# Weight sums moved from GpSimd to VectorE, and the modulation dots dealt anew, in a two-layer diffusion step

## The chip, the cores and the metric

One core of a Trainium2 chip runs the whole program. The metric is the device time of one execution in microseconds (us). Five engines work beside each other, each through its own queue in program order: TensorE (PE, with its weight loads as PEld), VectorE (DVE), ScalarE (ACT), GpSimd (POOL) and SyncE (SP, which only issues transfers here).

## The reference

Two layers are applied to 640 tokens of width 1024: 128 context tokens and 512 latent tokens, which differ in their conditioning vector. Each layer is a SwiGLU feed-forward network (FFN) with half weight, a token mixer of four branches (pooling, spatial gating, latent attention, short convolution), and a second FFN:

```python
def swiglu(h, w_gu, w_dn):
    g, u = jnp.split(h @ w_gu, 2, axis=-1)
    return (jax.nn.silu(g) * u) @ w_dn

def layer(x, cond, l, P, ctx, rope):
    mods = (jax.nn.silu(cond) @ P['w_mod'][l] + P['b_mod'][l]).reshape(Bc, N_MOD, 1, D_MODEL)
    ...
    f = swiglu(pre(x, 0), P['w_ffn_gu'][l, 0], P['w_ffn_dn'][l, 0])
    x = x + 0.5 * mods[:, 2] * rmsnorm(f, P['g_post'][l, 0])
    ...
```

`mods` are nine vectors of 1024 per layer and kind of token: scales, shifts and gains. Their matrix `w_mod` is 1024 x 9216 per layer. The hidden width of an FFN is 2816, which is 22 chunks of 128. Everything is float32.

## The kernel before

**Number format.** A float32 operand is split into two parts, h and lo (`split`, L240 to L243): ScalarE casts it to h (L242), VectorE subtracts h from it to get lo (L243). A product is then three matmuls: h by h, lo by h, h by lo. Weights are split as they stream in, so each weight tile costs a cast on ScalarE and a subtraction on VectorE. The halves are called wh and wl for weights, and the FFN's hidden values are split in the same way into `act`.

**An FFN.** The 22 chunks are worked in four parts (`PARTS`: 5, 5, 6, 6). The first part computes gate and up for each chunk by plain products (`gate`, `up`). The chunks of the other parts, but for the last two, are `block` tasks (L648): 15 in each of the four FFNs, 60 in all, in runs of 5, 6 and 4. After each of the first three parts come eight `down` tasks (L799 to L809), one for each 128 output columns: the part's hidden values times the down weights, copied out by ScalarE (L804) and added to a buffer in DRAM by a GpSimd transfer (L806, L808). `before` is the place in the list at which the first part's downs end; these eight are called the first downs here, the sixteen others the later downs.

**A block.** Gate and up for both halves of the tokens would be eight half-size products; a block does seven (Strassen's scheme). The operands' sums S1 to S4 are made once per FFN (`sums` at L627, during the end of the first part and the first downs). The weights' sums are made for every block: from the gate weights g and the up weights u, tiles of 128x1024, four adds of 128x512:

```python
add(t[:, one], g[:, one], u[:, one])          # L236
add(t[:, two], t[:, one], u[:, two])          # L237
add(u[:, one], u[:, one], u[:, two])          # L238
add(g[:, two], g[:, two], e["t"][:, two])     # L220
```

They run on GpSimd. A block's weights are four pieces, split in the order b (g as loaded), t (the tile `wt`), u (the tile `ru` after L238) and 4 (the second half of g after L220). L220 is issued behind the split of b, since that split reads g as loaded. The other three (method `sums`, L227) are issued behind the split of u of the block before, if the next g and u have been fetched by then, or else just ahead of the split of b. `make_piece` (L203) issues all of this; `advance` runs it ahead of the use: within block n the pieces of block n+1 are split, and the sums of block n+2 are made.

A block's TensorE order is: X from b; ScalarE copies X into Z (L672); Y from S1 and t; X from S2; Z from b's second half; X from S3 and u; Y from S4; X from the piece 4. Each is twelve matmuls of 320 columns. X, Z and Y are PSUM tiles; there are four such tiles. VectorE's order within the block, beside the splits, is: L682 (gate, first half), L684, the block's dots, L688 and L689 (up, first half, from Y), L693 and L694 (second half). The split of the finished hidden values is put off until after the next block's first product.

**Dots.** `w_mod` is not multiplied on TensorE, but for a few columns at the start: 128 of its columns at a time are loaded as a tile `wm` of 512 KB, and VectorE takes a product-and-sum of it with each of the two conditioning vectors (`dots`, L371, L375). Such a pair of passes is called a dot here. 96 dots are dealt over the tasks of the four FFNs (32, 28, 28 and 8). At L828 each kind of task has a room, L829 scales the first downs' room, and L833 gives each task its share of the FFN's dots by rounding the running sum. A task issues its dots after its own work (`side`); a block issues them between L684 and L688 (`mod_steps(sides[j])`, L686). The loads run two dots ahead in three buffers, issued by SP (L369) in one queue with the weight loads (L194, L195, L199); a load into a buffer waits there for the dot that read it last.

Of the kernel before, what the change touches and what calls it, by code (L numbers as in the profile page):

```python
# [80 lines left out]
class Kernel:  # L81
# [121 lines left out]
    def make_piece(self, p):  # L203

        nc = self.nc
        e = p.env
        g, u = e["g"], e["u"]
        one, two = slice(0, HK), slice(HK, 2 * HK)
        add = nc.gpsimd.tensor_add
        if p.kind == "4":  # L210
            h, lo = (self.fp.tile([P, HK], F32R, tag=t, name=self.nm(t)) for t in ("wh2", "wl2"))
            self.split(h, lo, g[:, two])
            return h, lo
        if p.kind == "b":
            self.sums(p)
        h = self.unit_tile(False, 2 * HK, F32R, "wh")
        lo = self.unit_tile(False, 2 * HK, F32R, "wl")
        self.split(h, lo, {"b": g, "t": e["t"], "u": u}[p.kind])
        if p.kind == "b":
            add(g[:, two], g[:, two], e["t"][:, two])  # L220
        if p.kind == "u":
            for q in self.streams[False]["raw"]:
                if isinstance(q, Piece) and q.kind == "b":
                    self.sums(q)
        return h, lo

    def sums(self, p):  # L227

        e = p.env
        if "t" in e:  # L230
            return
        g, u = e["g"], e["u"]
        one, two = slice(0, HK), slice(HK, 2 * HK)
        add = self.nc.gpsimd.tensor_add
        t = e["t"] = self.fp.tile([P, 2 * HK], F32, tag="wt", name=self.nm("wt"))
        add(t[:, one], g[:, one], u[:, one])  # L236
        add(t[:, two], t[:, one], u[:, two])  # L237
        add(u[:, one], u[:, one], u[:, two])  # L238
# [352 lines left out]
    def ffn(self, l, st, mod_todo, first=False):  # L591

        a, nc = self.a, self.nc
# [13 lines left out]
        def spill():  # L607

            nc.gpsimd.dma_start(self.d_x, self.x)
            self.gens["sums"] = sums()  # L610
# [155 lines left out]
        mid = []  # L766
        if first:
            def first_fn(*ws):
                p = [self.ps() for _ in ws]
                self.projs(list(zip(p, ws)), KC, self.h, (0, 1), hook=self.first_hook)  # L770
                self.advance(False, 5)
                self.st.close()
                begin()
                self.gens["sums"] = sums()
                new_act(0)
                gate_out(0, p[0], (0, 1))
                up_out(0, p[1], (0, 1))
                gate_out(1, p[2], (0, 1))
            mid.append(Task("first", first_fn, (wg[0, 0], wg[0, 1], wg[1, 0]), ahead=0))
            mid.append(up(1, 1, (0, 1)))  # L780
# [3 lines left out]
        for part, nj in enumerate(PARTS):  # L784
# [26 lines left out]
            before = before or len(mid)  # L811
# [13 lines left out]
            return Task("down2", fn, (wd[c][:, j0 * P:NJ * P],))  # L825


        room = {"gate": 1.4, "up": 1.4, "down": 1.0, "block": 1.0}  # L828
        rooms = [room.get(t.name, 0.0) * (0.3 if t.name == "down" and i < before else 1.0) for i, t in enumerate(mid)]  # L829
        done, n = 0.0, 0  # L830
        for t, x in zip(mid, rooms):
            done += x
# [592 lines left out]
    def build(self):  # L1425
# [6 lines left out]
        def start():  # L1432
# [77 lines left out]
            def squares():  # L1510
                sums = (acc, self.s6())
                for c in range(KC):
                    q = sums[c] if c < 2 else self.t6()
                    nc.scalar.activation(q, self.x[:, c, :], AF.Square)
                    if c > 1:
                        nc.vector.tensor_add(sums[c % 2], sums[c % 2], q)
                nc.vector.tensor_add(acc, *sums)
# [199 lines left out]
```

## Time and profile before

| | |
|---|---|
| Three timed runs | 3231.4, 3232.16, 3234.57 us; median 3232.16 |
| The profiled execution | 3228.82 us |
| its span, first to last instruction | 3227.0 us |
| Busy: TensorE | 3042.9 us, 94% |
| Busy: VectorE | 2334.3 us, 72% |
| Busy: ScalarE | 1436.4 us, 45% |
| Busy: GpSimd | 1079.7 us, 33% |
| TensorE's granted clock, mean | 0.981 of full speed |

Durations and waits below are of the profiled execution. A row of a wait names who stood, at which line, for whom, and how long. A matmul's time of 0.31 us includes its way through the array; such matmuls start about 0.147 us apart.

### The profile page before, as it was taken

The page shows a single profiled execution, that of the slowest core. Times are in us where ns is not written, and L with a number is a line of the kernel's source. Part 1 is how long each engine was busy: PE and PEld are TensorE (multiplying, and loading weights), DVE is VectorE, ACT ScalarE, POOL GpSimd, SP SyncE. Part 2 cuts the span into 40 slices and gives each one's busy share as a digit, 9 for nine tenths or more (in the row PEclk, how much of TensorE's full clock was granted, in tenths as well). Part 3 has the DMA queues.
Part 4 walks back from the last instruction along what each step waited for, and adds up shares of the span by engine and source line. Part 5 has one row for each costly group of instructions (what it writes and reads, how often), then busy time and mean ns, then how long its engine had stood idle before and what let it go on. Part 6 is the DMA issues. An engine that isn't in the chain of part 4 may idle for free. (4 is left out here: it accounts for less than half of the span.)

```text
span 3227.0 us, 51500 instructions
## 1 busy us (share of the span) xinstructions
PE 3042.9 (94%) x20278; PEld 2986.2 (93%) x20278; DVE 2334.3 (72%) x3282; ACT 1436.4 (45%) x2535; POOL 1079.7 (33%) x841
## 2 busy tenths in 40 slices
PE   7999998999999989999989999989999999899997
PEld 6999998899999979999979999979999998899997
DVE  7878768876666597787686788678666666866665
ACT  4344356454432354343554343564444324544344
POOL 4245344500011244354444354344000113343344
PEclk9999999999999999999999999999999999999999
DMA  4436653311234444536544436542111444345344
GB/s 178 166 110 186 165 169 119 133 58 60 68 112 148 154 150 158 158 118 175 181 152 157 151 119 179 180 152 93 60 55 61 144 140 163 139 133 140 104 130 153
DMA packets 140213, 433.45 MB, mean 134 GB/s; under 512 B 16834, under 2 KB 34050, under 8 KB 139076
## 3 DMA queue, kind: packets, MB, share of 16 engines
q1 hardware_dynamic: 119380, 351.34, 32.6%
q0 software_dynamic: 20304, 78.66, 9.1%
q8 instruction: 159, 2.61, 0.3%
q14 instruction: 82, 0.67, 0.1%
q10 hardware_dynamic: 288, 0.17, 0.0%
HBM read 377.51 MB, written 52.59 MB: 133 GB/s over the span
## 5 line engine op out<-in xcount | busy, mean ns | idle before, releaser
L243 DVE TENSOR_TENSOR wl<-raw,wh 128x1024 fp32r<-128x1024 f32 (+3 forms) x525 | 645.0, 1231 | 432.5 <-ACT wh L242 425.2
L311 PE MATMUL ps<-act,wh 128*128 128x320 f32 x2816 | 570.1, 313 | 29.5 <-DVE act L243 10.8
L242 ACT CAST wh<-raw 128x1024 fp32r<-128x1024 f32 (+3 forms) x525 | 481.2, 919 | 78.9 <-PE ps L311 39.1
L311 PEld LDWEIGHTS ps<-act,wh 128*128 128x128 f32 x2816 | 457.7, 190 | 38.2 <-DVE act L243 14.1
L665 PE MATMUL ps<-s,wh 128*128 128x320 f32 x1920 | 445.4, 311 | 26.7 <-DVE t L689 26.7
L375 DVE CUSTOM_DVE_ANT_0 t<-wm,sc,par 128x1024 bf16<-128x1024 f32 x256 | 373.2, 1493 | 10.0 <-DMA wm<-in_w_mod 9.9
L311 PE MATMUL ps<-slotA,wh 128*128 128x320 f32 x1312 | 366.4, 317 | 14.3 <-ACT wh L242 11.7
L311 PE MATMUL ps<-slotD,wh 128*128 128x320 f32 x1312 | 352.4, 316 | 20.7 <-DVE slotD L1528 15.0
L311 PE MATMUL ps<-slotA,wl 128*128 128x320 f32 x1312 | 363.5, 315 | 6.3 <-DVE wl L243 6.0
L311 PE MATMUL ps<-slotB,wh 128*128 128x320 f32 x1312 | 362.2, 314 | 3.0 <-DVE slotB L509 1.6
L311 PE MATMUL ps<-slotC,wh 128*128 128x320 f32 x1312 | 352.5, 317 | 7.1 <-ACT wh L242 3.2
L665 PEld LDWEIGHTS ps<-s,wh 128*128 128x128 f32 x1920 | 327.0, 188 | 32.8 <-ACT ps L672 22.2
L311 PE MATMUL ps<-act,wl 128*128 128x320 f32 x1408 | 355.0, 311 | 0.0
L665 PE MATMUL ps<-s,wl 128*128 128x320 f32 x960 | 298.0, 310 | 1.8 <-DVE wl L243 1.4
L311 PEld LDWEIGHTS ps<-slotD,wh 128*128 128x128 f32 x1312 | 236.9, 193 | 23.9 <-DVE slotD L1528 16.3
L311 PEld LDWEIGHTS ps<-slotA,wh 128*128 128x128 f32 x1312 | 239.1, 192 | 17.4 <-ACT wh L242 12.7
L311 PEld LDWEIGHTS ps<-slotA,wl 128*128 128x128 f32 x1312 | 239.1, 192 | 11.2 <-DVE wl L243 10.0
L311 PEld LDWEIGHTS ps<-act,wl 128*128 128x128 f32 x1408 | 246.9, 190 | 0.2
L311 PEld LDWEIGHTS ps<-slotC,wh 128*128 128x128 f32 x1312 | 236.9, 193 | 9.1 <-ACT wh L242 3.5
L311 PEld LDWEIGHTS ps<-slotB,wh 128*128 128x128 f32 x1312 | 239.0, 192 | 4.7 <-DVE slotB L509 2.1
L311 PE MATMUL ps<-slotC,wl 128*128 128x320 f32 x960 | 240.5, 316 | 1.4 <-DVE wl L243 1.0
L804 ACT COPY s<-ps 128x640 f32<-128x640 f32 x96 | 66.6, 694 | 297.0 <-issue 171.9
(341 smaller groups left out, 6461.9 us busy)
## 6 DMA issues: line engine op xcount, KB each, us to landing
raw<-in_w_gu SPq DMA_DIRECT2D x162, 512.0 KB, 3.8
wm<-in_w_mod SPq DMA_DIRECT2D x144, 512.0 KB, 4.7
raw<-in_w_dn SPq DMA_DIRECT2D x96, 384.0 KB, 3.2
raw<-in_w_gate SPq DMA_DIRECT2D x64, 512.0 KB, 3.6
d_f<-s POOLq DMA_DIRECT2D x96, 320.0 KB, 5.0
ru<-in_w_gu SPq DMA_DIRECT2D x60, 512.0 KB, 4.0
raw<-in_w_in SPq DMA_DIRECT2D x44, 512.0 KB, 3.4
raw<-in_w_dn SPq DMA_DIRECT2D x64, 320.0 KB, 2.9
```

The source lines that it names most:

```text
L242: self.nc.scalar.copy(h, src)
L243: self.nc.vector.tensor_sub(lo, src, h.bitcast(F32))
L311: nc.tensor.matmul(ps[:, hf, :HW], st[:, ws], m[:, k0 + k, hf * HW:(hf + 1) * HW], start=(first and k == 0 and i == 0), stop=(last and k = ...
L375: self.nc.vector.tensor_tensor_reduce(junk, wm, self.sc[:, j, :], 0.5, self.par[l][:, C_BMOD + ch:C_BMOD + ch + 1], ALU.mult, ALU.add, sel ...
L665: nc.tensor.matmul(o, w[x][:, ws], a[y][:, k, :], start=(new and k == 0 and i == 0), stop=(k == n - 1 and i == 2), skip_group_check=not new)
L804: nc.scalar.copy(t.rearrange("p (a b) -> p a b", a=2), ps[:, :, :HW])
```

## The change

The four weight sums of a block go from GpSimd to VectorE; where they are issued does not move. The rooms that deal the dots change: a block's room falls from 1.0 to 0.2, and the factor of the first downs rises from 0.3 to 0.6. The number of dots, their order and their loads stay.

```diff
@@ make_piece
-        add = nc.gpsimd.tensor_add
+        add = nc.vector.tensor_add
@@ sums
-        add = self.nc.gpsimd.tensor_add
+        add = self.nc.vector.tensor_add
@@ ffn
-        room = {"gate": 1.4, "up": 1.4, "down": 1.0, "block": 1.0}
-        rooms = [room.get(t.name, 0.0) * (0.3 if t.name == "down" and i < before else 1.0) for i, t in enumerate(mid)]
+        room = {"gate": 1.4, "up": 1.4, "down": 1.0, "block": 0.2}
+        rooms = [room.get(t.name, 0.0) * (0.6 if t.name == "down" and i < before else 1.0) for i, t in enumerate(mid)]
```

## Rows read from the trace of the kernel before

**Rows 1.** The page's first part: busy time, share of the span, instructions.

```profile
PE 3042.9 (94%) x20278; PEld 2986.2 (93%) x20278; DVE 2334.3 (72%) x3282; ACT 1436.4 (45%) x2535; POOL 1079.7 (33%) x841
```

**Rows 2.** Twelve block stages: window, length; busy PE, PEld, DVE, ACT, POOL; PEclk, DMA, GB/s.

```profile
1861.40:1941.80 80.40, 75.46 (x505) 73.85 (x505) 69.74 (x88) 36.39 (x59) 40.56 (x23) 1.00 0.38 120
...
2866.80:2928.90 62.10, 62.02 (x423) 61.64 (x422) 46.45 (x57) 30.16 (x49) 27.26 (x19) 1.00 0.26 83
...
sum 777.90, PE 749.31 PEld 740.65 DVE 639.62 ACT 362.93 POOL 368.64; mean PE 62.44 PEld 61.72 DVE 53.30 ACT 30.24 POOL 30.72
```

**Rows 3.** ScalarE's timeline, last FFN: start, length, what; two copies L672, one block apart.

```profile
2893.74 0.41 ACT L672 COPY ps<-ps 128x320 f32<-128x320 f32 x1 [0.81 <-PE ps L665]
...
2906.06 0.41 ACT L672 COPY ps<-ps 128x320 f32<-128x320 f32 x1 [0.81 <-PE ps L665]
```

**Rows 4.** TensorE's waits: total us, times, longest.

```profile
PE ps L665 <- DVE t L689: 26.7, 23, 2.4
```

**Rows 5.** VectorE's timeline in a block with a dot.

```profile
1389.09 1.27 DVE L375 CUSTOM_DVE_ANT_0 t<-wm,sc,par 128x1024 bf16<-128x1024 f32 x1
...
1390.29 2.30 DVE L375 CUSTOM_DVE_ANT_0 t<-wm,sc,par 128x1024 bf16<-128x1024 f32 x1
...
1393.05 0.49 DVE L689 TENSOR_TENSOR t<-t,ps 128x320 f32<-128x320 f32 x1
...
1395.23 1.07 DVE L694 TENSOR_TENSOR t<-t,t 128x320 f32<-128x320 f32 x1
...
1396.23 0.68 DVE L243 TENSOR_TENSOR wl<-raw,wh 128x512 fp32r<-128x512 f32 x1
...
1397.10 0.82 DVE L243 TENSOR_TENSOR act<-t,act 128x640 fp32r<-128x640 f32 x1 [0.19 <-ACT act L242]
```

**Rows 6.** TensorE's and GpSimd's timeline at the same place.

```profile
1393.68 0.39 PE L665 MATMUL ps<-s,wh 128*128 128x320 f32 x1 [2.39 <-DVE t L689]
...
1391.59 2.13 POOL L237 TENSOR_TENSOR wt<-wt,ru 128x512 f32<-128x512 f32 x1
```

**Rows 7.** Groups by form, GpSimd: busy, mean ns, idle before; two of four sums.

```profile
L237 POOL TENSOR_TENSOR wt<-wt,ru 128x512 f32<-128x512 f32 x60 | 129.0, 2149 | 4.7
...
L220 POOL TENSOR_TENSOR raw<-raw,wt 128x512 f32<-128x512 f32 x60 | 87.5, 1458 | 178.1 <-DVE wl L243 111.8 <-issue 66.4
```

**Rows 8.** VectorE's timeline in a first down, GpSimd idle: two passes of a dot.

```profile
1264.68 1.28 DVE L375 CUSTOM_DVE_ANT_0 t<-wm,sc,par 128x1024 bf16<-128x1024 f32 x1
...
1265.89 1.28 DVE L375 CUSTOM_DVE_ANT_0 t<-wm,sc,par 128x1024 bf16<-128x1024 f32 x1
```

**Rows 9.** Two lines by source: shortest, median, longest ns, then first and last start.

```profile
L694 DVE TENSOR_TENSOR t<-t,t x60: 491/1071/1078, 189.0 to 3135.6; 128x320 f32<-128x320 f32 x60
...
L243 DVE TENSOR_TENSOR wl<-ru,wh x60: 1212/1352/2603, 174.2 to 3121.8; 128x1024 fp32r<-128x1024 f32 x60
```

**Rows 10.** Three down stages by window, columns as in the block stages: first, then later.

```profile
1235.70:1275.50 39.80, 37.10 (x242) 36.58 (x241) 22.75 (x31) 14.62 (x22) 13.81 (x13) 0.96 0.53 184
...
1340.60:1375.80 35.20, 35.20 (x242) 35.20 (x242) 26.87 (x37) 11.79 (x17) 11.83 (x10) 1.00 0.85 243
...
1456.00:1498.20 42.20, 42.20 (x290) 42.20 (x289) 29.31 (x39) 12.32 (x17) 13.53 (x11) 1.00 0.77 213
```

**Rows 11.** First FFN, gates and ups: window; then timelines at its first down.

```profile
88.00:132.00 44.00, 44.00 (x302) 44.00 (x301) 42.81 (x57) 13.94 (x19) 10.61 (x5) 1.00 0.42 135
...
138.03 0.81 DVE L243 TENSOR_TENSOR act<-t,act 128x640 fp32r<-128x640 f32 x1
...
138.90 0.90 PE L311 MATMUL ps<-act,wh 128*128 128x320 f32 x2 [4.39 <-DVE act L243]
```

**Rows 12.** Transfers 1340 to 1376 us: KB, us to landing; then VectorE's idle before L375.

```profile
wm<-in_w_mod SPq DMA_DIRECT2D x7, 512.0 KB, 5.7
...
  DMA wm<-in_w_mod: 9.9, 10
```

## The prediction, made before the changed kernel ran

> **What bounds the kernel now.** I read the page's busy line first: TensorE is busy for 94% of the span, VectorE for 72%, GpSimd for 33% [rows 1]. So time can be won only where TensorE stands, and the next view is the table by stage over the twelve stretches of block products (four FFNs, three parts each, 60 blocks). They last 777.9 us together; the shortest one of five blocks lasts 62.1 us, the longest one of six 80.4 us [rows 2]. What a block costs without a stop is read from ScalarE's timeline: its copy of X into Z (L672) comes once a block, and two such copies lie 2906.06 - 2893.74 = 12.32 us apart where no dot is near [rows 3]. 60 x 12.32 = 739.2 us, so 777.9 - 739.2 = 38.7 us is all that the blocks have to give. Of it, 26.7 us is one wait by name: TensorE on VectorE's L689, 23 times, 1.16 us each [rows 4].
>
> One dotted block shows why. VectorE begins the two passes of a dot at 1389.09; the first takes 1.27 us, the second 2.30 us, and L689 comes only at 1393.05 [rows 5]. TensorE, which had ended the last product of the block and the X product of the next, stands 2.39 us for L689, since the next Y is written into the PSUM tile that L689 reads [rows 6]. The second pass is long because GpSimd is inside a weight sum (L237) during it [rows 6]. The same slowing shows wherever VectorE reads two SBUF operands while GpSimd adds: L694 takes 0.49 us at least and 1.07 us in the median, a split of 1024 columns 1.21 us at least and up to 2.60 us [rows 9]. The four sums of a block take 1.46 to 2.15 us each on GpSimd, some 7 us together (the longest and the shortest of the four in [rows 7]).
>
> **The change part by part.** *Dots.* From the rooms at L828 and L829 and the rounding at L833, the 96 dots of all four FFNs are dealt so (before to after): gates and ups of the first FFN 7 to 9, first downs 7 to 19, blocks 38 to 12, later downs 44 to 56. By FFN the blocks go 11, 12, 12, 3 to 4, 4, 4, 0. No two of the 12 are in neighbouring blocks, and three are in the last block of a part, where no next Y waits: nine are left that can make one wait.
>
> *Sums.* Four adds of 128x512 go from GpSimd to VectorE, 240 in all. The trace has no such add on VectorE; the nearest row is the split of the same 512 columns with two fp32 SBUF inputs, 0.68 us [rows 5]. An instruction holds VectorE some 0.07 us less than it lasts: passes of 1.28 us start 1.21 us apart [rows 8]. So an add costs 0.61 us. The bounds are 0.61 and, if something still slowed it as L694 is slowed, 0.61 x 1.07/0.49 = 1.3 us; I take 0.61, because the thing that slowed L694 is exactly what leaves.
>
> *VectorE's load in a block afterwards,* with undisturbed durations: three splits of 1024 at 1.14 (1.21 less 0.07 [rows 9]), one of 512 at 0.61, the act split of 640 at 0.75, five passes over PSUM at 0.42 (L689's 0.49 less 0.07) and L694 at 0.42 [rows 5, 9]: 7.3 us. Four adds: 2.4 us, and 0.1 us by estimate for the one that reads its forerunner. Sum 9.8 of 12.32 us. A dot is 2 x 1.21 + 0.08 = 2.5 us [rows 8]; a dotted block has 12.3 of 12.32 us, so it just fits, and its neighbours take up what is late.
>
> *What is queued behind the adds.* Three of them (L236 to L238) stand behind the split of u and ahead of L693, L694 and the w4 split; the fourth (L220) between the split of b and L682. What TensorE needs first is L689, and both places have slack before it: a product is 12.32/7 = 1.76 us, S4 ends 1.76 us before the block does and the next Y starts 1.76 us after, so L688 and L689 (1 us together) may lie 2.5 us late. Without a dot they are on time. With one, adding up the queue (wl of b, L220, L682, L684, wl of t, 2.5 us of dot, L688, L689) brings L689 about 0.7 us too late. The bounds are 0 and the 1.16 us that a wait on L689 takes today [rows 4]. 9 x 0.7 = 6.3 us. L694 also comes about 2 us later, and with it the act split; the downs read act a block later, except behind a part's last block, which has no sums behind it. The adds need their raw and ru tiles landed, or VectorE itself would stand; the loads are issued about one block ahead, and nothing in the trace stands on them.
>
> *Starts of the parts.* Of the 38.7 us, 38.7 - 26.7 = 12 us are not waits on L689: shorter stops at the first block of a part, on splits that come after GpSimd's chain of four sums (some 7 us [rows 7]). On VectorE the chain is 2.5 us, so the splits are ready in time. I leave 1.5 us for all twelve parts; the bounds are 0 and 12.
>
> *Blocks, sum:* 739.2 + 6.3 + 1.5 = 747.0, against 777.9: 30.9 us won.
>
> *Downs.* A later down has 4.4 us (5 chunks) or 5.3 us (6 chunks) of TensorE; VectorE needs 0.75 to 0.9 us for the split and 2.5 us for a dot, at most 3.4 us. Today TensorE never stands in the later downs: busy 35.20 of 35.20 us with VectorE at 26.87 [rows 10]. Two more dots make 31.9 of 35.20. Weights are split two downs ahead, so the single down with two dots is covered by 8.8 us of finished weights. I cost it at nothing; without that cover each extra dot costs its 2.5 us. In the first downs VectorE is busy 22.75 of 39.80 us [rows 10]; four more dots make 32.8. The act split and the operand sums stand ahead of these dots in program order. Nothing.
>
> *Gates and ups of the first FFN.* Here there is no cover. From 88 to 132 us VectorE is busy 42.81 of 44.00 us [rows 11]. Two more dots are 5.0 us, 1.2 us of it fits, 3.8 us is carried along. TensorE has four PSUM tiles and weights two units ahead, so it stands only at the end: the first down already waits 4.39 us for the last act split, which ends at 138.84 [rows 11], and will wait 3.8 us more. Bounds 0 and 5.0.
>
> *DMA.* The same loads, more of them inside the downs: seven wm loads in a later part of 35 us today at 85% share and 243 GB/s [rows 10], each landing 5.7 us after issue [rows 12]; nine would add 1.05 MB, 4.3 us at that rate, against 5.3 us free. A load is issued two dots ahead, so 5.7 us is covered by 8.8 us. SP's queue holds the wm load until an earlier dot has ended, with the raw loads behind it; three raw tiles lie ahead. VectorE stood 9.9 us in all for wm [rows 12]. Nothing, bound 4.3 us in each of the four densest stages.
>
> *Sum:* -30.9 + 3.8 = -27.1 us on the profiled execution of 3228.8 us (span 3227.0), to some 3202. The three timed runs have their median 3.3 us above it; the same step from the median gives 3232.2 - 27 = **3205 us**.
>
> **One rule weighed.** VectorE is busy for 69.74 of 80.40 us in the fullest block stage [rows 2]. The Trainium skill, "Perfetto Trace Analysis", section "Optimizing Scalar/DVE Operations", says that work may be offloaded from a saturated VectorE to ScalarE or even GpSimd, and adds that between VectorE and GpSimd it might not help because they share an SBUF port. The first half speaks against this change and is the third rival below; the trace agrees with the second half, in the 2.30 us pass beside L237.
>
> **The rivals.**
> 1. *The denser downs take part of it back.* If transfers do not keep up, each of the four stages with nine dots grows by 4.3 us: 17 us, 3205 + 17 = 3222 us. For: 85% share. Against: 15% free and two dots of lead. It decides once a load takes over about 8.8 us to land. Chance 0.13.
> 2. *No change.* The twelve dots added to the first downs fall in front of the splits and operand sums that the first block of each part needs: 12 x 2.5 = 30 us, 3235 us, against 3232. For: these stages hold the longest waits for act. Against: 17 us of VectorE's time free there [rows 10]. Chance 0.10.
> 3. *Slower: VectorE becomes the bound in the blocks.* If an add costs 1.2 us there, twice its price (as splits beside GpSimd take twice), a block needs 12.1 of 12.32 us, nothing makes up for a dot (12 x 2.5 = 30 us), and in-order waits of some 0.5 us a block (30 us) come on top: +60 + 3.8 - 38.7 = +25, 3257 us. It decides when VectorE has more than 2.5 us of backlog at L688 block after block. For: 9.8 of 12.32 us leaves little. Against: the 0.68 us row. Chance 0.09.
> 4. *All of it is won* and the gates lose nothing: 3232 - 38.7 = 3193.5 us. Chance 0.08.
>
> **How the numbers follow.** Forecast 0.60 at 3205 (own range 3197 to 3217). The range 3194 to 3227 takes in rival 1, the upper end of rival 4 and the bounds of the dotted blocks, the parts' starts, the gates and the transfers. About 0.2% is what a measurement here can tell from no change. Faster by over 0.2%: forecast, rivals 1 and 4, 0.81; within: rival 2, 0.10; slower: 0.09.
>
> **What would show it.** Right: L689 nearly gone from TensorE's waits, block stages near 62 us (five blocks) and 74.5 (six), splits in blocks near 1.23 us, L694 at 0.49 us, later downs still 35.2 and 42.2 us, the wait of the first down up from 4.4 to some 8 us. Wrong: VectorE's adds well over 0.7 us, waits for splits inside the later downs, VectorE standing on wm or ru, or L689 waits that stay in blocks without a dot.

## The result

The changed kernel takes 3197.89 us in the median (3197.05 to 3201.47), the kernel before 3232.14 us beside it: a ratio of 0.9902, 95% interval 0.9890 to 0.9915, or 34 us less. The forecast was 3205 us, 27 us less, in a range from 3194 to 3227. The profiled execution took 3198.12 us, its span is 3196.3 us, 30.7 us shorter than before.

The twelve block stages of the kernel after, by window (length, then busy PE, PEld, DVE, ACT, POOL, clock, DMA share, GB/s); they answer to [rows 2]:

```profile
1840.10:1914.50 74.40, 74.38 (x506) 73.90 (x505) 62.37 (x93) 36.06 (x59) 0.86 (x1) 1.00 0.35 111
...
2841.30:2902.90 61.60, 61.60 (x422) 61.60 (x421) 47.39 (x70) 29.84 (x49) 0.54 (x1) 1.00 0.23 70
...
sum 743.60, PE 743.04 PEld 739.09 DVE 592.61 ACT 360.29 POOL 14.15; mean PE 61.92 PEld 61.59 DVE 49.38 ACT 30.02 POOL 1.18
```

743.6 us now, 777.9 before. The six-block stage fell from 80.4 to 74.4 us, the undisturbed five-block stage from 62.1 to 61.6. By its records TensorE is busy 743.04 of 743.60 us, but a matmul's record reaches past the start of the next, so that short stands do not show there. ScalarE's copy of X into Z, once a block, shows them (the dot runs between the first two of these copies):

```profile
1380.56 0.41 ACT L672 COPY ps<-ps 128x320 f32<-128x320 f32 x1 [0.81 <-PE ps L665]
...
1392.88 0.41 ACT L672 COPY ps<-ps 128x320 f32<-128x320 f32 x1 [0.81 <-PE ps L665]
...
1405.71 0.41 ACT L672 COPY ps<-ps 128x320 f32<-128x320 f32 x1 [0.81 <-PE ps L665]
```

12.32 us from copy to copy without a dot, 12.83 us behind one. The three stages of the last FFN, whose blocks have no dot now, take 61.6 + 73.9 + 49.3 = 184.8 us, exactly 15 times 12.32. So the 743.6 - 739.2 = 4.4 us that are left lie in the nine stages with dots.

GpSimd went from 368.64 to 14.15 us, and VectorE, which took over 240 adds, is less busy in the blocks than before (592.61 against 639.62 us), partly since 26 dots left them and partly since its instructions got shorter.

The wait of [rows 4] and the forms of VectorE's instructions after (shortest, median, longest in ns; then a group by form with its mean):

```profile
PE ps L665 <- DVE t L689: 0.4, 2, 0.2
...
L694 DVE TENSOR_TENSOR t<-t,t x60: 491/492/494, 191.5 to 3104.7; 128x320 f32<-128x320 f32 x60
...
L243 DVE TENSOR_TENSOR wl<-ru,wh x60: 1218/1226/1228, 177.9 to 3090.8; 128x1024 fp32r<-128x1024 f32 x60
...
L237 DVE TENSOR_TENSOR wt<-wt,ru 128x512 f32<-128x512 f32 x60 | 41.5, 692 | 2.1
```

L689 is waited for twice, 0.4 us in all (23 times and 26.7 us before). L694 takes 0.49 us always (median 1.07 in [rows 9]), the split of `ru` at most 1.23 us (up to 2.60), and an add 0.69 us, against 2.15 us on GpSimd in [rows 7].

A block with a dot, VectorE's timeline, in the same stage as [rows 5] but one block later, down to the next block's sums (L236 to L238):

```profile
1388.15 1.22 DVE L243 TENSOR_TENSOR wl<-wt,wh 128x1024 fp32r<-128x1024 f32 x1
...
1389.28 1.28 DVE L375 CUSTOM_DVE_ANT_0 t<-wm,sc,par 128x1024 bf16<-128x1024 f32 x1
...
1390.49 1.28 DVE L375 CUSTOM_DVE_ANT_0 t<-wm,sc,par 128x1024 bf16<-128x1024 f32 x1
...
1392.22 0.49 DVE L689 TENSOR_TENSOR t<-t,ps 128x320 f32<-128x320 f32 x1
...
1393.77 0.68 DVE L236 TENSOR_TENSOR wt<-raw,ru 128x512 f32<-128x512 f32 x1
...
1394.48 0.69 DVE L237 TENSOR_TENSOR wt<-wt,ru 128x512 f32<-128x512 f32 x1
...
1395.09 0.68 DVE L238 TENSOR_TENSOR ru<-ru 128x512 f32<-128x512 f32 x1
```

Both passes take 1.28 us. L689 ends at 1392.71 us, and TensorE's next Y starts at 1392.86 us, only 0.2 us later than it could have by the pace of its matmuls.

Two down stages after, columns as above, and the wm loads in the first of the two (KB, us to landing); they answer to [rows 10] and [rows 12]:

```profile
1330.80:1366.00 35.20, 35.20 (x243) 35.20 (x242) 30.22 (x50) 11.68 (x17) 5.98 (x7) 1.00 0.92 261
...
1440.70:1482.90 42.20, 42.20 (x290) 42.20 (x289) 35.12 (x55) 12.32 (x17) 6.00 (x7) 1.00 0.90 255
...
wm<-in_w_mod SPq DMA_DIRECT2D x9, 512.0 KB, 8.7
```

TensorE still never stands in them. But the share of the transfers rose from 0.85 to 0.92, and a wm load lands after 8.7 us (5.7 before).

The first FFN's first downs: the stage by window, before and after, then of the kernel after VectorE's timeline (a dot's second pass, the last act split) and TensorE's two stands; they answer to [rows 11]:

```profile
129.90:172.20 42.30, 37.89 (x242) 37.36 (x241) 24.75 (x33) 12.69 (x18) 14.34 (x12) 0.92 0.52 177
...
128.00:176.00 48.00, 38.34 (x242) 37.67 (x241) 37.37 (x58) 15.04 (x22) 7.97 (x9) 0.86 0.60 204
...
122.66 2.60 DVE L375 CUSTOM_DVE_ANT_0 t<-wm,sc,par 128x1024 bf16<-128x1024 f32 x1
...
141.90 0.81 DVE L243 TENSOR_TENSOR act<-t,act 128x640 fp32r<-128x640 f32 x1
...
137.47 0.90 PE L311 MATMUL ps<-act,wh 128*128 128x320 f32 x2 [5.80 <-ACT act L242]
...
142.76 1.43 PE L311 MATMUL ps<-act,wh 128*128 128x320 f32 x4 [3.86 <-DVE act L243]
```

TensorE stands 5.80 us and then 3.86 us, where it stood 4.39 us once. The stage takes 48.0 us; the same matmuls took 42.3 us before.

So the span's 30.7 us are -34.2 us in the blocks, +5.7 us in the first FFN's first downs, and -2.2 us in all other stages together. These 2.2 us are not traced to the change: the start of the first downs alone lies between 128.0 and 130.3 us in the profiles of this study, 130.0 us in the kernel before and in the run with lowered gate rooms.

### The profile page after: what moved, and what is told of

Same layout as the page of the kernel before. It is cut to its first block, busy times and chain, and to the rows that moved or that the text cites. A ratio compares the mean times of both kernels' runs of the same rounds, so it can differ in the third digit from the quotient of the medians.

```text
span 3196.3 us, 51354 instructions
## 1 busy us (share of the span) xinstructions
PE 3036.4 (95%) x20278; PEld 2985.0 (93%) x20278; DVE 2353.4 (74%) x3522; ACT 1432.2 (45%) x2535; POOL 653.7 (20%) x601
## 5 line engine op out<-in xcount | busy, mean ns | idle before, releaser
L243 DVE TENSOR_TENSOR wl<-raw,wh 128x1024 fp32r<-128x1024 f32 (+3 forms) x525 | 601.8, 1148 | 380.2 <-ACT wh L242 371.9
L375 DVE CUSTOM_DVE_ANT_0 t<-wm,sc,par 128x1024 bf16<-128x1024 f32 x256 | 330.2, 1327 | 12.9 <-DMA wm<-in_w_mod 12.5
L311 PEld LDWEIGHTS ps<-slotA,wh 128*128 128x128 f32 x1312 | 240.5, 193 | 19.9 <-ACT wh L242 15.1
L808 POOL DMA_DIRECT2D d_f<-s x64 | 55.3, 864 | 800.4 <-ACT s L804 720.7
```

Of the source, the lines that this page charges most:

```text
L243: self.nc.vector.tensor_sub(lo, src, h.bitcast(F32))
L311: nc.tensor.matmul(ps[:, hf, :HW], st[:, ws], m[:, k0 + k, hf * HW:(hf + 1) * HW], start=(first and k == 0 and i == 0), stop=(last and k = ...
L375: self.nc.vector.tensor_tensor_reduce(junk, wm, self.sc[:, j, :], 0.5, self.par[l][:, C_BMOD + ch:C_BMOD + ch + 1], ALU.mult, ALU.add, sel ...
L808: nc.gpsimd.dma_start(self.d_f[c], t, accum_op=ALU.add)
```

## The experiments

Ratios are to the kernel before, run on the same chip. Edits are shown against the changed kernel; "..." marks what is left out of a line. Where a kernel has lines more than the changed one, its line numbers are shifted, and the text says to what.

**The sums alone.** The dots are dealt as before.

```diff
-        room = {"gate": 1.4, "up": 1.4, "down": 1.0, "block": 0.2}
+        room = {"gate": 1.4, "up": 1.4, "down": 1.0, "block": 1.0}
-  ... * (0.6 if t.name == "down" and i < before else 1.0)
+  ... * (0.3 if t.name == "down" and i < before else 1.0)
```

> Sums on VectorE, dots dealt as before (38 of 96 in blocks). Theory A (both parts are needed: a dotted block fills VectorE, 9.8 + 2.5 of 12.32 us, so dotted blocks in a row pile up and L689 comes late): the blocks win well under the 34 us of the changed kernel, some 10 to 20 us, TensorE waits on L689 in most runs of dotted blocks, some 20 us in all; time about 3215 us. Rival B (GpSimd's adds beside the dots were the whole cause, so that moving them is enough): block stages as in the changed kernel, 744 us together, and the first FFN's gates as in the kernel before; time about 3193 us.

Measured: 3213.26 us, ratio 0.9950 (0.9933 to 0.9966). The blocks take 763.8 us, 14.0 us less than before; the first FFN's first downs 42.1 us, as before. The sum over its block stages, and TensorE's waits:

```profile
sum 763.80, PE 752.10 PEld 739.25 DVE 638.13 ACT 357.18 POOL 14.03; mean PE 62.68 PEld 61.60 DVE 53.18 ACT 29.76 POOL 1.17
```

```profile
PE ps L665 <- DVE t L689: 11.5, 15, 1.0
```

15 waits on L689 are left, up to 1.0 us each; 14 of them stand behind a block with a dot that follows another such block. Theory A holds, B falls: taking GpSimd away does not make 38 dotted blocks free, since a dotted block leaves VectorE late and the next dotted one finds it late.

**The dots alone.** The sums stay on GpSimd.

```diff
-        add = nc.vector.tensor_add
+        add = nc.gpsimd.tensor_add
...
-        add = self.nc.vector.tensor_add
+        add = self.nc.gpsimd.tensor_add
```

> Sums stay on GpSimd, dots dealt as in the changed kernel (12 in blocks). Theory A: a block without a dot runs in 12.32 us beside GpSimd, as it does in the last FFN of the kernel before; nine dots still cost 1.2 us each and the parts' first blocks their stops: blocks about 755 us together (777.9 before), first FFN's first downs 5 to 6 us longer as in the changed kernel; time about 3216 us. Rival B: the blocks stay near 778 us, time about 3236 us.

Measured: 3212.28 us, ratio 0.9946 (0.9931 to 0.9960). The blocks take 757.2 us, 20.6 us less than before; the first FFN's first downs 47.9 us. The sum over its block stages, and TensorE's waits:

```profile
sum 757.20, PE 747.44 PEld 742.28 DVE 602.15 ACT 364.38 POOL 345.66; mean PE 62.29 PEld 61.86 DVE 50.18 ACT 30.36 POOL 28.80
```

```profile
PE ps L665 <- DVE t L689: 7.9, 6, 2.1
```

Six long waits, four of 0.9 and two of 2.1 us, are a part of what the few dots left in the blocks still cost beside GpSimd. In the last FFN, where no block has a dot, the stages take the same 184.8 us as in the changed kernel: beside a block without a dot GpSimd's sums cost nothing here. Theory A again. The two halves won 14.0 and 20.6 us in the blocks, 34.6 together; the whole change won 34.2. They add up, although only 12 blocks with a dot are left for the sums to help, where there were 38; why they still win 13.6 us there is not shown. The loss of 5.7 us comes with the dots alone.

**Fewer dots in the first FFN's gates.**

```diff
-        room = {"gate": 1.4, "up": 1.4, "down": 1.0, "block": 0.2}
+        room = {"gate": 0.3, "up": 0.3, "down": 1.0, "block": 0.2}
-  ... * (0.6 if t.name == "down" and i < before else 1.0)
+  ... * (0.8 if t.name == "down" and i < before else 1.0)
```

> The changed kernel with rooms 0.3 (not 1.4) for gates and ups and 0.8 (not 0.6) for the first downs: the first FFN has 2 dots in its gates and ups instead of 9, none in the last two of them. Theory (the 5.7 us that the first FFN's first downs lost are dots queued ahead of the last act split): that stage falls from 48.0 to about 39 us, as long as in the other FFNs, the rest stays; time about 3189 us. Rival (the stage is longer for the dots dealt to its own downs): no gain or a loss, 3198 us or more, since these downs get 8 dots instead of 5.

Measured: 3189.73 us, ratio 0.9871 (0.9856 to 0.9885). The first downs by window, and the gates ahead of them:

```profile
130.20:165.40 35.20, 35.20 (x242) 35.20 (x241) 32.50 (x51) 12.59 (x18) 3.98 (x7) 1.00 0.70 250
...
88.00:128.00 40.00, 40.00 (x275) 40.00 (x274) 31.56 (x41) 13.28 (x18) 11.03 (x6) 1.00 0.27 87
```

The stage takes 35.2 us, less than the 39 us expected: TensorE does not stand in it at all, though these downs hold eight dots instead of five. In the gates VectorE is busy 31.56 of 40.00 us, where it was 42.81 of 44.00 before. So both stands of that stage, the 4.39 us of the kernel before among them, came from dots queued ahead of the last act split; dots in the downs themselves cost nothing here. The granted clock of the stage is 1.00, where it was 0.92 and 0.86 with the stands.

**No dots in the blocks of the last three FFNs, more in their downs.**

```diff
-        room = {"gate": 1.4, "up": 1.4, "down": 1.0, "block": 0.2}
+        room = {"gate": 1.4, "up": 1.4, "down": 1.0, "block": 0.2 if first else 0.0}
```

> The changed kernel with no dots at all in the blocks of the last three FFNs; their 28, 28 and 8 dots all lie in the downs, 11 in each of the later parts of eight downs with 28, three of them in pairs. Theory (the downs have room and the few dots in the blocks cost almost nothing): within 3 us of the changed kernel, 3195 to 3200 us; later downs 35.2 and 42.2 us as before. Rival (denser downs cost, by VectorE or by transfers): each of the four stages with 11 dots grows by several us, 3205 us or more.

Measured: 3202.25 us, ratio 0.9914 (0.9899 to 0.9929). The downs did keep their 35.2 and 42.2 us, but two of the block stages behind them grew, from 74.7 to 77.2 and from 74.4 to 78.2 us. VectorE at the end of the downs, and TensorE at the start of the first of these stages:

```profile
1362.14 1.29 DVE L375 CUSTOM_DVE_ANT_0 t<-wm,sc,par 128x1024 bf16<-128x1024 f32 x1 [3.04 <-DMA wm<-in_w_mod]
...
1371.90 1.28 DVE L375 CUSTOM_DVE_ANT_0 t<-wm,sc,par 128x1024 bf16<-128x1024 f32 x1
...
1372.04 0.41 PE L665 MATMUL ps<-s,wl 128*128 128x320 f32 x1 [2.25 <-DVE wl L243]
```

VectorE stood 3.04 us for a wm load that had not landed, its remaining dots moved on to the block's start, and TensorE stood 2.25 us for a split. The theory missed by where the price falls: not in the dense downs, but in the first block behind them. Eight fewer dots in the blocks win less than this costs. The two stages that grew are the six-block ones behind downs of 35.2 us; behind the downs of 42.2 us, also with 11 dots, nothing was lost. The interval of the ratio overlaps that of the changed kernel, 4 us apart in the medians, so the reading rests on the two block stages of the profile, +2.5 and +3.8 us.

**Two adds more in each block.** L236 and L237 are issued twice.

```diff
         add(t[:, one], g[:, one], u[:, one])
         add(t[:, two], t[:, one], u[:, two])
+        add(t[:, one], g[:, one], u[:, one])
+        add(t[:, two], t[:, one], u[:, two])
```

> The changed kernel with L236 and L237 issued twice: two adds of 128x512 more on VectorE in each block, 0.61 us each, same result. Theory (a block without a dot needs 9.8 of 12.32 us and L689 may lie 2.5 us late, so 1.3 us more is still covered; only dotted blocks fall behind): block stages 744 to 749 us, time within 5 us of the changed kernel, about 3201 us. Rival (VectorE's queue is already what a block waits for, and every add is paid): 60 x 1.25 = 75 us more, about 3273 us.

Measured: 3222.05 us, ratio 0.9977 (0.9968 to 0.9986), some 24 us more than the changed kernel ((0.9977 - 0.9902) x 3230). The blocks take 768.4 us. Both expectations missed. ScalarE's copy of X into Z (L674 here) in two neighbouring blocks without a dot:

```profile
1433.80 0.41 ACT L674 COPY ps<-ps 128x320 f32<-128x320 f32 x1 [0.81 <-PE ps L667]
...
1446.44 0.41 ACT L674 COPY ps<-ps 128x320 f32<-128x320 f32 x1 [0.81 <-PE ps L667]
```

12.64 us a block, not 12.32, once the first two or three blocks of a part have used up what they were ahead; blocks behind a dot take 14.2 to 15.1 us.

**Four adds more in each block.**

```diff
         add(t[:, one], g[:, one], u[:, one])
         add(t[:, two], t[:, one], u[:, two])
+        add(t[:, one], g[:, one], u[:, one])
+        add(t[:, two], t[:, one], u[:, two])
+        add(t[:, one], g[:, one], u[:, one])
+        add(t[:, two], t[:, one], u[:, two])
```

> The changed kernel with L236 and L237 issued three times: four adds more, 2.5 us a block, so that a block without a dot needs 12.3 of 12.32 us of VectorE. Theory: the point from which VectorE is the bound lies here; the short stands for ScalarE in each block no longer fit, and a dot (2.5 us) is paid in full: 9 x 2.4 us and some 0.2 to 0.5 us in each block, 20 to 50 us more, 3220 to 3250 us, with waits on L689 in most blocks. Rival (VectorE still has room): within 10 us of the changed kernel.

Measured: 3295.53 us, ratio 1.0206 (1.0189 to 1.0223), some 98 us more than the changed kernel, again outside both expectations. The blocks take 840.8 us. The same copy (L676 here), ScalarE's cast of the hidden values with what stands behind it, and TensorE's waits (L681 is L677 of the changed kernel, L688 is L684, L693 is L689, L698 is L694):

```profile
1461.02 0.41 ACT L676 COPY ps<-ps 128x320 f32<-128x320 f32 x1 [0.81 <-PE ps L669]
...
1466.15 0.72 ACT L246 CAST act<-t 128x640 fp32r<-128x640 f32 x1 [4.71 <-DVE t L698]
...
1467.09 0.43 ACT L681 COPY t<-ps 128x320 f32<-128x320 f32 x1
...
1475.12 0.41 ACT L676 COPY ps<-ps 128x320 f32<-128x320 f32 x1 [0.81 <-PE ps L669]
...
PE ps L669 <- ACT t L681: 54.4, 36, 2.7
...
PE ps L669 <- DVE t L688: 11.8, 12, 2.7
...
PE ps L669 <- DVE t L693: 7.5, 9, 1.0
```

14.10 us a block: the last two adds cost 14.10 - 12.64 = 1.46 us, all of their 0.72 us each. Taken back from there, four adds more at 0.72 us leave 14.10 - 2.88 = 11.2 us that VectorE's round of the changed kernel takes, stands included, and two adds on top make 12.66 us, against 12.64 measured. So the slack of an undotted block is some 1.1 us by this estimate, not the 2.5 us of the prediction's sum. And the wait is another one than I had looked for: mostly not L689, but ScalarE's copies. The adds stand ahead of L694; ScalarE's cast of the hidden values waits for L694 (4.71 us), and behind that cast, in ScalarE's queue, stand the copies of Y and X that free X for its third product.

**GpSimd's adds beside VectorE's.** VectorE makes the sums as in the changed kernel; GpSimd makes four adds a block of the same size, into a tile that nothing in the block reads.

```diff
             add(g[:, two], g[:, two], e["t"][:, two])
+            nc.gpsimd.tensor_add(self.wm[:, one], e["t"][:, two], self.sc[:, 0, one])
...
         add(u[:, one], u[:, one], u[:, two])
+        for _ in range(3):
+            self.nc.gpsimd.tensor_add(self.wm[:, one], t[:, two], self.sc[:, 0, one])
```

> The changed kernel, and GpSimd beside it does four adds of 128x512 a block into a tile that nobody reads, on operands of the same size (the sums that are used stay on VectorE). Theory (an add on GpSimd slows whatever reads two SBUF operands on VectorE): splits, sums and dots last up to twice as long while GpSimd is in an add, VectorE needs some 14 of 12.32 us a block, and the blocks become VectorE's: 60 x 1.5 to 2 us more, 3280 to 3320 us. Rival (GpSimd's sums mattered only because their results came late): as the changed kernel, 3198 to 3203 us.

Measured: 3311.60 us, ratio 1.0254 (1.0234 to 1.0275). The blocks take 858.6 us. VectorE's forms (the split of 512, the act split, L220, L694 as L697 here, and L239, which is L238) and GpSimd's adds:

```profile
L246 DVE TENSOR_TENSOR wl<-raw,wh 128x512 fp32r<-128x512 f32 x62 | 94.0, 1517 | 16.6 <-ACT wh L245 16.6
...
L246 DVE TENSOR_TENSOR act<-t,act 128x640 fp32r<-128x640 f32 x65 | 92.8, 1428 | 14.3 <-ACT act L245 14.3
...
L220 DVE TENSOR_TENSOR raw<-raw,wt 128x512 f32<-128x512 f32 x60 | 64.7, 1079 | 2.1
...
L697 DVE TENSOR_TENSOR t<-t,t 128x320 f32<-128x320 f32 x60 | 50.4, 840 | 2.1
...
L239 DVE TENSOR_TENSOR ru<-ru 128x512 f32<-128x512 f32 x60 | 41.0, 684 | 0.0
...
L241 POOL TENSOR_TENSOR wm<-wt,sc 128x512 f32<-128x512 f32 x180 | 296.1, 1645 | 306.8 <-DVE wt L238 297.1
```

The split of 512 columns takes 1.52 us in the mean (0.69 in the changed kernel), the act split 1.43 (0.83), L697 0.84 (0.49), L220 1.08 (0.69); L239, inside which GpSimd's first add starts, keeps its 0.68 us. GpSimd's results are used by nobody in the block, so the lateness of its results is out as a cause: it is the adds as such, beside VectorE, that hold VectorE up. (The added adds also read the tile of the sums, which VectorE overwrites a block later; VectorE never stands for that in this trace.)

**The changed kernel once more, and the operand sums on VectorE too.** The second has the lowered gate rooms of the third experiment, and one line more:

```diff
-                    nc.gpsimd.tensor_add(d, f(self.h[0][:, c, :]), f(self.h[1][:, c, :]))
+                    nc.vector.tensor_add(d, f(self.h[0][:, c, :]), f(self.h[1][:, c, :]))
```

> The changed kernel once more, unaltered, beside the next one on the same chip: 0.990 of the kernel before, some 30 us less.

> The kernel with the gates' rooms lowered, and the operand sums' adds too (L637, 32 of 128x640, at the end of the first part) on VectorE. Theory (a GpSimd add beside VectorE costs VectorE more than VectorE's own add): the weight split ahead of the last act split falls from 1.76 to 0.82 us, the first downs of the last three FFNs from 39.8 to about 37 us; 6 to 12 us less than with the lowered rooms alone, ratio to the kernel before about 0.984. Rival (VectorE's queue in front of the act split grows by the adds): no gain or some us more, ratio 0.988 or above.

Measured: 3196.02 us, ratio 0.9891 (0.9875 to 0.9908) for the changed kernel again; 3178.27 us, ratio 0.9837 (0.9822 to 0.9851) with the operand sums on VectorE.

In the second profile of the changed kernel one six-block stage takes 1.4 us more than in the first. Its window, and VectorE near its start:

```profile
1840.64:1916.50 75.86, 74.68 (x506) 73.92 (x505) 63.30 (x96) 36.17 (x59) 0.86 (x1) 1.00 0.35 110
...
1843.64 1.28 DVE L375 CUSTOM_DVE_ANT_0 t<-wm,sc,par 128x1024 bf16<-128x1024 f32 x1 [1.84 <-DMA wm<-in_w_mod]
```

A dot of the downs ahead, which hold 9, stood 1.84 us for its load and ran on into the first block, as in the run with 11; TensorE stands 1.2 us for L684 a little later. So with 9 dots such a part loses something in one execution and nothing in another.

VectorE's timeline ahead of the last act split, in the kernel with the lowered rooms alone and in that with the operand sums on VectorE, then TensorE's wait on weight casts in both:

```profile
1225.87 1.76 DVE L243 TENSOR_TENSOR wl<-raw,wh 128x640 fp32r<-128x640 f32 x1
...
1227.55 0.48 DVE L243 TENSOR_TENSOR act<-t,act 128x320 fp32r<-128x320 f32 x1
```

```profile
1223.93 0.82 DVE L243 TENSOR_TENSOR wl<-raw,wh 128x640 fp32r<-128x640 f32 x1
...
1224.66 0.49 DVE L243 TENSOR_TENSOR act<-t,act 128x320 fp32r<-128x320 f32 x1
```

```profile
PE ps L311 <- ACT wh L242: 18.2, 6, 5.1
```

```profile
PE ps L311 <- ACT wh L242: 13.3, 6, 3.2
```

The split fell from 1.76 to 0.82 us as expected, and the time to the ratio expected. But the place was another: the first downs of the last three FFNs take 119.2 us together and took 119.7. The gain lies in the stretches ahead of them, from the last block of one FFN to the first downs of the next: some 6.5 of the 9.0 us between the two profiles. 4.9 us of it is the wait on weight casts, and what shortened that wait was not taken apart; the longest one, 5.1 us in the kernel with the lowered rooms, is 3.6 us in the changed kernel, so that a part may be that one profile's own. This is the fastest kernel of the study.

## Why the prediction was right, and where it was off

**What bounds the kernel.** Right. The blocks had 38.7 us to give by the count of 60 times 12.32 us, and gave 34.2; the blocks without a dot reach the 12.32 us.

**The wait and its cause.** Right, and shown from both sides: the dots alone and the sums alone each take more than half of the L689 waits away, and adds on GpSimd bring the slowing back. The sum that makes the pass of 2.30 us long is not L237, though, but the one ahead of it:

```profile
1389.30 2.21 POOL L236 TENSOR_TENSOR wt<-raw,ru 128x512 f32<-128x512 f32 x1 [1.22 <-DVE wl L243]
```

L236 starts inside the first pass, which keeps its 1.27 us. The second pass begins inside L236 and ends at 1392.59 us, 1.08 us behind the end of L236 (1391.51 us); L237, begun inside that pass, ends 1.13 us behind it. They take turns: whichever of the two begins second mostly waits until the other is through.

**The price of an add.** 0.61 us was right for an add that does not read its forerunner (L238 starts 0.61 us behind L237; L237, which does read L236, starts 0.71 us behind it). The bound of 1.3 us was not needed, and the third rival's 1.2 us an add did not come.

**The dotted blocks.** Right in kind, somewhat oversized: 6.3 us forecast (0.7 in each of nine). TensorE's waits on L689 show only 0.4 us, but the nine stages with dots last 4.4 us more than 12.32 us a block, 0.2 to 0.8 us each, a start of a part with 0.3 us among them. L689 comes later, as forecast; the next Y starts some 0.2 us late, and the rest is lost in short steps further on in that block.

**VectorE's load.** 9.8 of 12.32 us was a sum of instructions, without the stands that the order forces: 0.19 us before the act split and about 0.8 us before the split of b, each for a cast on ScalarE. The round takes 11.2 us by the estimate above; the 0.4 us that are still missing were not itemized. Nothing came of it here, since four adds still fit, but that L689 may lie 2.5 us late was the wrong point from which VectorE decides: two adds more already cost 24 us, and with four most of the waiting is for ScalarE's copies, behind L694 and ScalarE's cast. I had written that L694 comes later and that only the downs read what follows. The copies behind that cast were left out; the wait for them is the one that takes over.

**Starts of the parts.** I left 1.5 us for all. In the last FFN they cost nothing (184.8 us, as above); with the dotted blocks 4.4 us is left in all, instead of 7.8.

**The first FFN.** Right in kind, mis-sized: +3.8 us forecast, +5.7 measured, above the bound of 5.0. A dot of the second pair ran beside GpSimd's operand sum (L637) and took 2.60 us in its second pass (the row at 122.66 us of VectorE's timeline), and TensorE, standing longer, was granted 0.86 of its clock in the mean of the stage, 0.92 before.

**Downs and transfers.** Right in the first profile, but the margin was used up: loads land 8.7 us after issue, against the 8.8 us of lead that I gave as the point from which the first rival decides. VectorE stood 12.5 us for wm (9.9 before) and 2.4 us for ru, which I had named as a sign of being wrong, and in the second profile one stage lost 1.4 us by it. With the denser parts the first rival did decide, at 2.5 and 3.8 us in two stages rather than 4.3 us in all four. The second rival did not come: the first downs of the last three FFNs take 119.6 us together, 119.2 before.

**The rule weighed.** With 38 dotted blocks the four sums cost 14 us more in the blocks on GpSimd than on VectorE; four adds a block on GpSimd beside a VectorE that makes the sums cost 115 us (858.6 against 743.6). The Trainium skill, "Perfetto Trace Analysis", section "Optimizing Scalar/DVE Operations", says that work may be offloaded from a saturated VectorE to GpSimd, but that this might not help because the two share an SBUF port. The first half would have kept the sums where they were; the runs bear out the second.

**The sum.** -30.9 + 3.8 = -27.1 forecast; -34.2 + 5.7 - 2.2 = -30.7 measured on the profiled executions, -34 in the medians. The blocks came out 3.3 us better than forecast and the first FFN 1.9 us worse, so that two errors partly cancel. Of the 7 us by which the median came out under the forecast, some 3.5 us are the choice of executions: the profiled one before lay 3.3 us under its median, the one after 0.2 us above.

## What to carry to other kernels

An add on GpSimd is not free for VectorE: where both read two operands from SBUF, price it by what VectorE's instructions lose beside it, and compare this with VectorE's own add. Here 0.69 us on VectorE stood against 2.15 us on GpSimd, with VectorE's next instruction held up; but where VectorE had room, in blocks without a dot, GpSimd's sums cost nothing. When work is put into a queue that still has room by its busy share, add the stands that its order forces before you call the rest slack, and follow every instruction that comes later into the queues of the other engines, not only to its own reader. Work without a due time belongs where the busy engine waits for nothing of it: the dots cost most just ahead of a split that a stage's first matmuls need.

## What the runs showed of the hardware that I had not expected

Beside each other a dot's pass goes from 1.28 to 2.30 us and an add of GpSimd from 1.29 (L220 at 1386.79 us of the kernel before) to 2.2 us. It is not both engines at half speed but turns: the one that is running keeps its time (the first pass beside L236, L239 in the run with added adds), and the one that begins beside it is the longer by the wait. In the run with GpSimd's adds beside VectorE's, the instructions of VectorE on two SBUF operands that begin inside such an add end, four in five of them, at the add's end plus their own undisturbed length, less 0.12 to 0.14 us. Passes with one operand in PSUM (L689, 0.49 us) stay the same. The Trainium skill, "GPSIMD Engine Reference", "Key points", names contention with VectorE instructions that have two SBUF inputs; the runs agree, and show that the contention is a wait of up to the other's whole instruction.

The two halves of a change that meet in the same wait added up almost exactly, 14.0 + 20.6 against 34.2 us; no run shows why.
